# A two-block transformer kernel: the causal convolution by even and odd tokens, without matmuls

## The chip, the cores and the metric

One NeuronCore of one Trainium2 chip. The time is device microseconds of one execution; of a kernel the median of its runs is given. The engines are named as in the profile: PE is TensorE (PEld its weight loads), DVE is VectorE, ACT is ScalarE, POOL is GpSimd, SP only issues DMAs. The profile is one execution with its own time.

## The reference, cut to what matters

Two blocks over 1024 tokens of width 1024, float32. The first is the one that the change is about; each block ends in a convolutional feed-forward net, and the second has attention in place of these two branches.

```
h  = rms_norm(x, even_norm_g)
z  = h @ even_w_in + even_b_in                     # 1024 -> 4 * 512
za, zb = gelu(z[:, :1024]), z[:, 1024:]
# branch A: u, v = split(za); v = layer_norm(v); mixed = per head and 128-token chunk w_s @ v + b_s
ya = u * mixed
# branch B: a, g = split(zb)
c  = causal_dwconv(a * sigmoid(g), conv_w, conv_b) # 31 taps, one filter for each of 512 channels
yb = silu(layer_norm(c))
x  = x + concatenate([ya, yb], -1) @ even_w_out
```

## The kernel before

Every product is made three times, since each operand is split in a high and a low part (`split`: ACT casts the high part, DVE subtracts it): `mm3` issues high*high, high*low, low*high into one PSUM bank (`bank`, eight of them).

The order on every engine is the order in which the code issues. `Ticker` keeps a program time: a tick is called after every two k-steps, that is six matmuls of 512 columns, `after(n, fn)` issues `fn` n ticks later, and hooks run at each tick. An engine takes its own list in order and waits at each instruction for what it needs. `Meter` keeps a rough backlog of DVE and POOL, by a cost for each instruction and a credit for each tick.

`mix` is the first block's first half. Its stages on PE, in order:
1. `psu` for branch B: for each of four channel tiles c (128 channels each) the products for a and g; `done` makes `h` = (a + bias) * sigmoid(g), channels on partitions, 1024 tokens along the row.
2. `psv`: the products for v, token tile by token tile (`i` of 8); `v_chain` has the bias, gelu, layer norm and the split (`vn`, `vh`, `vl`).
3. `psu` for u, and between them `mix_pair(c)`: the mixing products (`psm`), bias on ACT (`mixed`), transposes (`pst`), `u * pst` on DVE, and the split into `ya`.
4. `psd`: `ya` times the first four row tiles of `w_out`, in two groups of two, each over 16 units (8 token tiles, 2 halves); DVE adds each finished bank to `x` (`x<-psd,x`).
5. `yb_chain`: transposes of the convolved channels (`psc`), layer norm, transposes back (`psb`), silu and split (`ybh`, `ybl`); then `psd` for the last four row tiles of `w_out`, and the norm of the feed-forward net (`psn`).

The 31 taps of the convolution run in the background of stages 1 to 4 (`background`, at each tick). A tap at distance s adds w * h, s tokens later, to `acc`:
- on DVE: one `scalar_tensor_tensor` on up to 1024 tokens, issued while DVE's backlog is below `slack`;
- by DMA: ACT multiplies (`tap`), and POOL's DMA queue adds the product to `sides` in HBM (an accumulating DMA); when a tile has all of them, `close` loads the sum (`side`), and POOL adds it to `acc`. `DMA_TAPS` = (6, 10, 9, 7) of each tile go this way;
- on PE: 12 taps of the last tile, as products with diagonal matrices (`diagonals`, `pe_taps`, tile `psk`), put into stage 2 ahead of token tile 2.

`yb_chain` is issued `YB_AT` ticks after the last convolution instruction is. `weights.take` hands out the split weights of a group and sets the splits of the next one.

## Time and profile before

| | |
|---|---|
| median of 3 runs | 2198.48 us (2198.35 to 2198.55) |
| profiled execution | 2198.7 us; its span 2197.0 us |
| PE busy | 2172.1 us, 99% of the span |
| DVE, ACT, POOL busy | 1591.7, 1094.8, 771.0 us (72, 50, 35%) |
| mean granted clock of PE | 0.998 of full |
| mean DMA rate | 164 GB/s |

Busy time is the union of an engine's instructions. Matmuls overlap: one of 512 columns is listed with about 390 ns, and the next starts 227 ns after it, so what one costs is read from start to start. `mix` takes the first 300 us.

### The profile page before, as it was taken

To read this page: it belongs to the slowest core of one execution; us is meant where nothing else is said; L and a number is where in the kernel's file an instruction comes from. 1 tells how busy PE (TensorE), PEld (TensorE's weight loads), DVE (VectorE), ACT (ScalarE), POOL (GpSimd) and SP (SyncE) were. 2 spreads that over 40 slices of the span, in tenths; PEclk is the share of its full clock that TensorE was granted. 3 is DMA by queue.
4 is the path that set the end of the run, shared out by engine and by line. 5 is a ranking of instruction groups with operands and counts; after the bars stand their busy time and mean duration, and the time that the engine had idled before them with its cause. 6 is when DMAs were issued, how large, how long until landed. Compare 5 with 4: busy or idle time off the path is not lost.

```text
span 2197.0 us, 29344 instructions
## 1 busy us (share of the span) xinstructions
PE 2172.1 (99%) x10496; PEld 1822.3 (83%) x10496; DVE 1591.7 (72%) x2551; ACT 1094.8 (50%) x1667; POOL 771.0 (35%) x561
## 2 busy tenths in 40 slices
PE   8999999999999999999999999999999999999998
PEld 7888788888888888888888888888888888888887
DVE  6998859877777775555777667776787777777556
ACT  5445455444444445254555655554654444444532
POOL 1122134766666330041112221211466666653001
PEclk9999999999999999999999999999999999999999
DMA  5569422434444597356344444743134444349933
GB/s 193 130 129 192 149 87 72 165 147 158 172 151 157 190 368 284 137 180 163 101 116 113 125 129 122 239 145 117 68 125 168 163 158 173 134 158 351 364 130 123
DMA packets 140850, 359.48 MB, mean 164 GB/s; under 512 B 16672, under 2 KB 17056, under 8 KB 140704
## 3 DMA queue, kind: packets, MB, share of 16 engines
q1 hardware_dynamic: 134512, 335.15, 45.0%
q0 software_dynamic: 5040, 18.27, 4.3%
q10 hardware_dynamic: 1152, 4.19, 0.5%
q8 instruction: 82, 1.34, 0.2%
q14 instruction: 64, 0.52, 0.1%
HBM read 219.68 MB, written 104.31 MB: 147 GB/s over the span
## 4 chain that ended last, share of the span: by engine, by line
PE 48%; issue 9%; DVE 2%; DMA 2%; ACT 2%; POOL 1%; SPq 1%; POOLq 0%; DVEq 0%; ACTq 0%
PE psd L1273 9%; PE psu L273 4%; PE psu L274 4%; PE psu L272 4%; PE psb L1093 3%; PE psb L1090 3%; PE psb L1091 3%; PE po L1594 3%; PE psc L1093 2%; PE psc L1090 2%; PE psc L1091 2%; PE ppt L1575 1%; PE pss L1508 1%; PE pss L1507 1%; PE ppt L1574 1%
## 5 line engine op out<-in xcount | busy, mean ns | idle before, releaser
L1273 PE MATMUL psd<-ab 128*128 128x512 f32 x1800 | 410.4, 390 | 0.0
L1273 PEld LDWEIGHTS psd<-ab 128*128 128x128 f32 x1800 | 337.6, 188 | 70.4 <-DVE ab L142 0.7
L272 PE MATMUL psu<-hTh,w 128*128 128x512 f32 (+1 forms) x608 | 239.9, 395 | 0.0
L273 PE MATMUL psu<-hTl,w 128*128 128x512 f32 (+1 forms) x608 | 232.1, 382 | 1.1 <-DVE hTl L142 1.1
L274 PE MATMUL psu<-hTh,w 128*128 128x512 f32 (+1 forms) x608 | 232.1, 382 | 0.0
L210 ACT CAST ab<-ab 128x1024 fp32r<-128x1024 f32 x150 | 156.0, 1051 | 140.3 <-PE psd L1273 54.5
L142 DVE TENSOR_TENSOR ab<-ab,ab 128x1024 fp32r<-128x1024 f32 x150 | 192.8, 1338 | 36.1 <-ACT ab L210 35.7
L142 DVE TENSOR_TENSOR x<-psd,x 128x512 f32<-128x512 f32 x152 | 101.5, 686 | 133.6 <-PE psd L1273 108.4
L142 POOL TENSOR_TENSOR y<-y,y 128x512 f32<-128x512 f32 x66 | 93.4, 1415 | 184.6 <-DMA act<-y 109.9
L1127 ACT COPY sn<-psb 128x512 f32<-128x512 f32 x120 | 70.4, 586 | 165.6 <-PE psb L1093 121.8
L142 DVE TENSOR_TENSOR tt<-ppt,tt 128x512 fp32r<-128x512 f32 (+1 forms) x160 | 101.4, 635 | 64.4 <-ACT tt L210 62.8
L210 ACT CAST tt<-ppt 128x512 fp32r<-128x512 f32 (+1 forms) x160 | 86.6, 541 | 113.4 <-PE ppt L1575 73.0
L274 PEld LDWEIGHTS psu<-hTh,w 128*128 128x128 f32 x608 | 115.1, 189 | 22.4
L273 PEld LDWEIGHTS psu<-hTl,w 128*128 128x128 f32 x608 | 115.6, 190 | 18.1 <-DVE hTl L142 1.9
L142 POOL TENSOR_TENSOR sm<-sm,mhalf 128x1 f32<-128x1 f32 (+2 forms) x38 | 33.2, 875 | 276.4 <-DVE sm L142 274.0
L272 PEld LDWEIGHTS psu<-hTh,w 128*128 128x128 f32 x608 | 115.5, 190 | 16.6 <-ACT hTh L210 0.2
L142 POOL MEMSET tt<- 128x256 f32 x64 | 19.8, 312 | 308.6 <-PE ppt L1575 110.5
L142 POOL TENSOR_TENSOR s<-wr 128x512 f32<-128x512 f32 x40 | 86.5, 2162 | 110.6 <-DVE psa L142 97.9
L142 DVE TENSOR_TENSOR wl<-wr,wh 128x1024 fp32r<-128x1024 f32 x88 | 116.0, 1318 | 0.5 <-ACT wh L210 0.5
L1594 PE MATMUL po<-tt,v 128*128 128x256 f32 x640 | 109.0, 292 | 4.0 <-DVE tt L142 4.0
L1524 ACT ACTIVATE p<-p,sma 128x896 f32<-128x896 f32 (+7 forms) x128 | 99.5, 778 | 25.6 <-DVE sma L142 25.0
L142 DVE TENSOR_TENSOR pse<-psc,sn 128x512 f32<-128x512 f32 x40 | 28.0, 699 | 115.6 <-ACT sn L1127 110.7
(252 smaller groups left out, 5896.2 us busy)
## 6 DMA issues: line engine op xcount, KB each, us to landing
wr<-in_w_up_dram SPq DMA_DIRECT2D x88, 512.0 KB, 4.3
ab<-act SPq DMA_DIRECT2D x154, 256.0 KB, 5.4
act<-y SPq DMA_DIRECT2D x66, 512.0 KB, 3.1
wq<-in_w_down_dram SPq DMA_DIRECT2D x44, 512.0 KB, 5.1
wt<-wq SPq DMA_DIRECT2D x44, 512.0 KB, 4.6
ab<-wt SPq DMA_DIRECT2D x88, 256.0 KB, 5.4
ab<-in_w_down_dram SPq DMA_DIRECT2D x66, 256.0 KB, 5.4
wr<-in_w_qkv_dram SPq DMA_DIRECT2D x24, 512.0 KB, 4.3
```

Of the source, the lines that this page charges most:

```text
L142: return fn(*args, **kw)
L210: nc.scalar.copy(hi, src)
L272: nc.tensor.matmul(out_ap, st[0], mv[0], start=first, stop=False)
L273: nc.tensor.matmul(out_ap, st[0], mv[1], start=False, stop=False)
L274: nc.tensor.matmul(out_ap, st[1], mv[0], start=False, stop=last)
L1090: nc.tensor.matmul(ps, st[0], mv[0], start=f, stop=False, skip_group_check=True)
L1091: nc.tensor.matmul(ps, st[0], mv[1], start=False, stop=False, skip_group_check=True)
L1093: nc.tensor.matmul(ps, st[1], mv[0], start=False, stop=e, skip_group_check=True)
L1127: nc.scalar.copy(self.sn[key], self.b)
L1273: nc.tensor.matmul(ps, a[:, c], b[:, HALF:D], start=first and k == 0, stop=last and k == 2, skip_group_check=True)
L1524: nc.scalar.activation(p, p, AF.Exp, bias=sm[:, 2:3], scale=0.125, accum_out=lsum[hp][:, c:c + 1])
L1594: nc.tensor.matmul(po[:, c], v2[:, kb, :], tt[:, z, 256 * n:256 * n + 256], start=(g == 0 and n == 0 and z == 0), stop=(g == j and n == 1 ...
```

## The change

The tokens of `h` are kept in two halves, even (h0) and odd (h1), and so are the taps: W0 at even distances (16), W1 at odd ones (15). With y0 = W0 * h0 and y1 = W1 * h1 in the two halves of `acc`, and cc = (W0 + W1) * (h0 + h1), the even outputs are y0 + y1 one step later, the odd ones cc - y0 - y1. Each filter runs over 512 tokens.
- y0 and y1: 29 taps for each tile on DVE (`tap`) and their first ones on ACT (`start`). The `acc` of three tiles is stored to HBM (`park`) and loaded again.
- cc: all 16 taps by DMA, two in one transfer of 512 KB (`send`), 8 transfers for each tile, as many in all as before (32). The sum is loaded by SP, and four DVE instructions put the output `y` together (`merge`), in place of POOL's addition.
- `pe_taps`, `diagonals` and their splits are gone.
- The mixing products are set by ticks (`MIX_AT`, `MIX_STEPS`), between the u's; ya's products are one group of four row tiles: half as many additions to `x`. Its first four units (`YA_HEAD`) do three of the four row tiles first.
- The two layer norm steps of a `vn` pair alternate; `Meter`'s numbers, slacks and weight splits are set anew, one of them in attention (`W_O_AT`).

What the change moves, at the three places that the prediction speaks of. PE, stage 2, after the products of token tile 1 (`psv`), before:

```order
L273 MATMUL psv_1042<-w_927,hTh_165 128x512
L274 MATMUL psv_1042<-w_927,hTl_166 128x512
L508 MATMUL psk_1077<-hh_984,dgh_745 128x512
L508 MATMUL psk_1077<-hl_985,dgh_745 128x512
L508 MATMUL psk_1077<-hh_984,dgl_746 128x512
L508 MATMUL psk_1077<-hh_984,dgh_745 128x510
```

PE at the same place after the change:

```order
L282 MATMUL psv_1099<-w_972,hTh_165 128x512
L283 MATMUL psv_1099<-w_972,hTl_166 128x512
L281 MATMUL psv_1138<-w_871,hTh_161 128x512
L282 MATMUL psv_1138<-w_871,hTh_161 128x512
L283 MATMUL psv_1138<-w_871,hTl_162 128x512
```

All 72 products of `psk` are gone, and the next token tile follows at once. PE, stage 4, ahead of the first `psc` (of the convolved channels `acc`, later `y`), before:

```order
L274 MATMUL psd_1976<-w_1674,ya_1717 128x512
L272 MATMUL psd_1976<-w_1759,ya_1814 128x512
L273 MATMUL psd_1976<-w_1759,ya_1814 128x512
L274 MATMUL psd_1976<-w_1759,ya_1814 128x512
L779 MATMUL psc_1986<-ident,acc_540 128x128
L779 MATMUL psc_1986<-ident,acc_665 128x128
L779 MATMUL psc_1986<-ident,acc_827 128x128
```

PE ahead of the first `psc` after the change:

```order
L281 MATMUL psd_2039<-w_1793,ya_1835 128x512
L282 MATMUL psd_2039<-w_1793,ya_1835 128x512
L283 MATMUL psd_2039<-w_1793,ya_1835 128x512
L862 MATMUL psc_2050<-ident,y_1736 128x128
L862 MATMUL psc_2050<-ident,y_1921 128x128
L862 MATMUL psc_2050<-ident,y_1962 128x128
L862 MATMUL psc_2050<-ident,y_2020 128x128
```

`psc` stood behind 60 of the 192 products of ya, and stands now behind 90. DVE, the last convolution instructions, before (the last tap is that on `acc_983`):

```order
L142 SCALAR_TENSOR_TENSOR acc_983<-h_907,cw_108,acc_983 128x996
L142 SCALAR_TENSOR_TENSOR acc_983<-h_907,cw_108,acc_983 128x995
L142 TENSOR_TENSOR x_1843<-psd_1850,x_1843 128x512
L142 SCALAR_TENSOR_TENSOR acc_983<-h_907,cw_108,acc_983 128x994
L142 TENSOR_TENSOR x_1843<-psd_1871,x_1843 128x512
L142 TENSOR_TENSOR w_1867<-wr_1703,w_1867 128x1024
```

DVE's last convolution instructions after the change (tile 3's `merge`, from `cc_1969` to `y_2020`):

```order
L151 TENSOR_TENSOR x_1773<-psd_1953,x_1773 128x512
L151 TENSOR_TENSOR x_1948<-psd_1988,x_1948 128x512
L151 TENSOR_TENSOR x_1948<-psd_2002,x_1948 128x512
L151 TENSOR_TENSOR cc_1969<-cc_1969 128x512
L151 TENSOR_TENSOR cc_1969<-acc_1243 128x512
L151 TENSOR_TENSOR y_2020<-acc_1243 128x511
L151 TENSOR_TENSOR y_2020<-cc_1969 128x512
L151 TENSOR_TENSOR x_1948<-psd_2024,x_1948 128x512
```

The taps ended on DVE among the first two additions to `x`, and POOL added the sums; now the last four instructions of `merge` stand behind six additions and wait for SP's load of `cc_1969`.

The diff, cut to its core:

```
-DMA_TAPS = (6, 10, 9, 7)
-PE_TAPS = 12
-PE_TAPS_AT = 2
-DIAG_AT = 40
+NP2 = (CONV_W + 1) // 2
+PAD = NP2
+DMA_PAIRS = (8, 8, 8, 8)
 DMA_PACE = 3
 CLOSE_AT = 6
 MERGE_STEPS = 6
-YB_AT = 3
-T_SLACK = 3.5
-DMA_STEPS = 8
+YB_AT = 2
+T_SLACK = 5.0
+DMA_STEPS = 6
...
-MIX_LAG = 8
+MIX_AT = 17
+MIX_STEPS = 4
+W_OUT_AT = (1, 4, 5, 6)
+W_OUT2_AT = (17, 20, 23, 26)
+YA_HEAD = 4
+YA_HI = 3
+BASE_AHEAD = 2
+PARK_AT = 2
+PARKED = 3
+LOAD_LEFT = (12, 8, 4, 2)
+W_O_AT = (1, 3, 11)
...
-            self.backlog += self.fixed + self.per_elem * n
+            fixed = self.fixed + 0.06 * (name == "scalar_tensor_tensor" or n < 64)
+            self.backlog += fixed + self.per_elem * n
...
-    vec = Meter(nc.vector, 0.12, 1.06e-3)
+    vec = Meter(nc.vector, 0.10, 1.05e-3)
     pool = Meter(nc.gpsimd, 0.12, 2.25e-3)
-    tk.hooks.append(lambda: (vec.step(1.28), pool.step(1.3)))
+    tk.hooks.append(lambda: (vec.step(1.36), pool.step(1.3)))
...
-        def take(self, spread, delay=0):
+        def take(self, spread, delay=0, at=None):
...
-                    after(1 + delay + i * spread, self.split_next)
+                    after(at[i] if at else 1 + delay + i * spread, self.split_next)
...
+        def part(u, js):
+            i, t = u
+            sl = slice(t * HALF, (t + 1) * HALF)
+            for j in js:
+                ah, al = acts[j]
+                a = ah(i), al(i)
+                if j == 0:
+                    banks[u] = bank("psd")
+                mm3(banks[u], a, (ws[j][0][:, sl], ws[j][1][:, sl]), j == 0, j == n - 1)
+                if j % 2 == 1 and j < n - 1:
+                    yield
+        def close(u):
+            i, t = u
+            sl = slice(t * HALF, (t + 1) * HALF)
+            ps = banks.pop(u)
+            after(1, lambda: vec.tensor_tensor(to[i][:, sl], ps, xs[i][:, sl], op=ALU.add))
+        for u in units[:head]:
+            yield from part(u, range(n - 1))
+            if n % 2 == 0:
                 yield
+        for m, u in enumerate(units[:head]):
+            yield from part(u, (n - 1,))
+            close(u)
+            if m % 2 == 1:
+                yield
+        for u in units[head:]:
+            yield from part(u, range(n))
+            close(u)
+            yield
+            if then is not None and u[1] == 1:
+                after(1, lambda i=u[0]: then(i))
...
+        accs, convs, cc_at, ccs, dma_todo, dma_last, dma_left = {}, {}, {}, {}, {}, {}, {}
+        conv_todo, merge_todo = deque(), deque()
+        slack = [2.0]
+        sides = dpool.tile([NC4, P, 2, HALF], F32, tag="sides", name="sides")
+        parks = dpool.tile([PARKED, P, 2, HALF], F32, tag="parks", name="parks")
...
+        class Conv:
+            def __init__(self, c):
+                self.c = c
+                self.h = stile([P, 2, HALF], name="h")
+                self.acc = None
+                self.todo = [(f, k) for k in range(1, NP2) for f in range(2) if 2 * k + f < CONV_W]
...
+            def add_phases(self):
+                c = self.c
+                t = stile(name="x2")
+                self.x2, self.ws, self.b2 = (t[:, a:b] for a, b in ((0, PAD + HALF), (D - NP2, D),
+                                                                    (D - NP2 - 1, D - NP2)))
+                pool.memset(self.x2[:, :PAD], 0.0)
+                pool.tensor_copy(self.ws[:, 0:1], cw[:, c, 0:1])
+                pool.tensor_tensor(self.ws[:, 1:], pairs[:, c, :, 0], pairs[:, c, :, 1], op=ALU.add)
+                pool.tensor_tensor(self.b2, cb[:, c:c + 1], cb[:, c:c + 1], op=ALU.add)
+                vec.tensor_tensor(self.x2[:, PAD:], self.h[:, 0, :], self.h[:, 1, :], op=ALU.add)
+            def start(self):
+                if self.acc is None:
+                    self.acc = stile([P, 2, HALF], name="acc")
+                    nc.scalar.activation(self.acc[:, 0, :], self.h[:, 0, :], AF.Identity,
+                                         bias=cb[:, self.c:self.c + 1], scale=self.weight(0, 0))
+                    nc.scalar.activation(self.acc[:, 1, :], self.h[:, 1, :], AF.Copy,
+                                         scale=self.weight(1, 0))
+            def tap(self):
+                self.start()
+                f, k = self.todo.pop(0)
+                t = self.acc[:, f, k:]
+                vec.scalar_tensor_tensor(t, self.h[:, f, :HALF - k], self.weight(f, k), t,
+                                         op0=ALU.mult, op1=ALU.add)
...
+            def park(self):
+                nc.gpsimd.dma_start(parks[self.c], self.acc)
+                self.acc = None
+            def send(self, n):
+                c, x2 = self.c, self.x2
+                t = stile([P, 2, HALF], name="tap")
+                for z in range(2):
+                    k = 2 * n + z
+                    bias = {"bias": self.b2} if k == 0 else {}
+                    nc.scalar.activation(t[:, z, :], x2[:, PAD - k:PAD - k + HALF],
+                                         AF.Identity if k == 0 else AF.Copy,
+                                         scale=self.ws[:, NP2 - 1 - k:NP2 - k], **bias)
                 def add():
+                    if n == 0:
                         nc.gpsimd.dma_start(sides[c], t)
                     else:
+                        nc.gpsimd.dma_start(sides[c], t, accum_op=ALU.add)
+                    dma_left[c] -= 1
                 after(1, add)
+            def merge(self, step):
+                y0, y1 = self.acc[:, 0, :], self.acc[:, 1, :]
+                q0, q1 = ccs[self.c][:, 0, :], ccs[self.c][:, 1, :]
...
+                elif step == 0:
+                    vec.tensor_tensor(q0, q0, q1, op=ALU.add)
+                elif step == 1:
+                    vec.tensor_tensor(q1, y0, y1, op=ALU.add)
+                elif step == 2:
+                    self.y = stile(name="y")
+                    self.out = self.y.rearrange("p (m f) -> p f m", f=2)
+                    nc.scalar.copy(self.out[:, 0, 0:1], y0[:, 0:1])
+                    vec.tensor_tensor(self.out[:, 0, 1:], y0[:, 1:], y1[:, :HALF - 1], op=ALU.add)
+                else:
+                    vec.tensor_tensor(self.out[:, 1, :], q0, q1, op=ALU.subtract)
+                    accs[self.c] = self.y
...
+        def queue_conv(cv):
+            cv.add_phases()
+            convs[cv.c] = cv
+            conv_todo.append(cv)
+            dma_todo[cv.c] = deque(lambda n=n: cv.send(n) for n in range(DMA_PAIRS[cv.c]))
+            dma_left[cv.c], dma_last[cv.c] = DMA_PAIRS[cv.c], tk.t
...
-            while conv_todo and vec.backlog < slack[0]:
-                conv_todo.popleft()()
+            for c in range(NC4):
+                if c not in cc_at and dma_left.get(c) == 0 and tk.t >= dma_last[c] + CLOSE_AT:
+                    left = sum(len(cv.todo) for cv in conv_todo)
+                    if left <= LOAD_LEFT[c] and len(merge_todo) <= 2:
+                        cc_at[c] = tk.t
+                        ccs[c] = stile([P, 2, HALF], name="cc")
+                        nc.sync.dma_start(ccs[c], sides[c])
+                        if c < PARKED:
+                            convs[c].acc = stile([P, 2, HALF], name="acc")
+                            nc.sync.dma_start(convs[c].acc, parks[c])
+                        steps = [-k for k in range(2 * DMA_PAIRS[c], NP2)] + list(range(4))
+                        merge_todo.extend((convs[c], step) for step in steps)
+                    break
+            while vec.backlog < slack[0] and sum(hT.done) == NT:
+                if merge_todo and tk.t >= cc_at[merge_todo[0][0].c] + MERGE_STEPS and not merge_todo[0][0].todo:
+                    cv, step = merge_todo.popleft()
+                    cv.merge(step)
+                elif conv_todo:
+                    cv = conv_todo[0]
+                    if len(cv.todo) <= BASE_AHEAD and len(conv_todo) > 1:
+                        conv_todo[1].start()
+                    cv.tap()
+                    if not cv.todo:
+                        conv_todo.popleft()
+                else:
+                    break
         tk.hooks.append(background)
...
-                    st["sig"], st["h"] = stile(name="sig"), stile(name="h")
+                    st["sig"], st["cv"] = stile(name="sig"), Conv(c)
                 nc.scalar.activation(st["sig"][:, sl], outs[(1, t)], AF.Sigmoid,
                                      bias=b_in[:, 12 + c:13 + c])
+                def phases(ap):
+                    return ap.rearrange("p (m f) -> p f m", f=2)
                 vec.scalar_tensor_tensor(
-                    st["h"][:, sl], outs[(0, t)], b_in[:, 8 + c:9 + c], st["sig"][:, sl],
+                    st["cv"].h[:, :, t * 256:(t + 1) * 256], phases(outs[(0, t)]),
+                    b_in[:, 8 + c:9 + c], phases(st["sig"][:, sl]),
                     op0=ALU.add, op1=ALU.mult)
                 if t == 1:
-                    queue_conv(c, st["h"])
+                    queue_conv(st["cv"])
...
+            def c():
+                for e in range(2):
+                    y = zs[:, e, :]
+                    vec.scalar_tensor_tensor(y, y, sm[:, 12 + 2 * e:13 + 2 * e], vgb[:, 0, :],
+                                             op0=ALU.subtract, op1=ALU.mult)
+                for e in range(2):
+                    y = zs[:, e, :]
+                    vec.scalar_tensor_tensor(y, y, sm[:, 22 + e:23 + e], vgb[:, 1, :],
+                                             op0=ALU.mult, op1=ALU.add)
...
-            if i == PE_TAPS_AT:
-                pe_taps()
...
-            after(MIX_LAG + 1, a)
-            after(MIX_LAG + 2, b)
-            after(MIX_LAG + 4, d)
-            after(MIX_LAG + 5, e)
+                def fin():
+                    yh, yl = hpair([P, S], "ya")
+                    hi_of(yh, u)
+                    after(1, lambda: lo_of(yl, u, yh))
+                    yas[c] = tok_view(yh, yl)
+                after(YA_HI if c < NC4 - 1 else 1, fin)
+            for n, fn in enumerate((a, b, None, d)):
+                if fn:
+                    after(MIX_AT + MIX_STEPS * c + n, fn)
+            return e
+        mixed_at = tk.t
+        ends = [mix_pair(c) for c in range(NC4)]
...
                 if t == 1:
-                    mix_pair(c)
-            ws = weights.take(2)
+                    after(max(1, mixed_at + MIX_AT + MIX_STEPS * c + 4 - tk.t), ends[c])
             if c < NC4 - 1:
+                ws = weights.take(2)
                 after(U_NEXT, weights.split_next)
+            else:
+                weights.lo_at = 1
+                ws = weights.take(0, at=W_OUT_AT)
+                load_x(0)
             drive(up_units(hT, ws, outs, done))
...
-        load_x(0)
-        for ks in ((0, 1), (2, 3)):
-            tk.until(lambda: all(k in yas for k in ks))
-            if ks[0] == 0:
-                for i in range(1, NT):
-                    after(max(1, 2 * i - X_AHEAD), lambda i=i: load_x(i))
-            down_group([yas[k] for k in ks], weights.take(4), xs)
+        for i in range(1, NT):
+            after(max(1, 4 * i - X_AHEAD), lambda i=i: load_x(i))
+        def ya_view(c):
+            def pick(part):
+                def view(i):
+                    tk.until(lambda: c in yas)
+                    return yas[c][part](i)
+                return view
+            return pick(0), pick(1)
+        down_group([ya_view(c) for c in range(NC4)], weights.take(0, at=W_OUT2_AT), xs, head=YA_HEAD)
...
-        return g + [rows(io["w_out"], ks) for ks in ((0, 1), (2, 3), (4, 5, 6, 7))]
+        return g + [rows(io["w_out"], ks) for ks in ((0, 1, 2, 3), (4, 5, 6, 7))]
```

More of the change, by code (lines that the diff above doesn't have):

```diff
@@ L444, in drive, with down_units @@
             tick()
-    def down_units(acts, ws, xs, then=None, to=None, tiles=range(NT)):
+    def down_units(acts, ws, xs, then=None, to=None, tiles=range(NT), head=0):
         to = to or xs
         n = len(ws)
-        for i in tiles:
-            for t in range(2):
-                sl = slice(t * HALF, (t + 1) * HALF)
-                ps = bank("psd")
-                for j in range(n):
-                    ah, al = acts[j]
-                    mm3(ps, (ah(i), al(i)), (ws[j][0][:, sl], ws[j][1][:, sl]),
-                        j == 0, j == n - 1)
-                    if j % 2 == 1 and j < n - 1:
-                        yield
-                after(1, lambda i=i, sl=sl, ps=ps: vec.tensor_tensor(
-                    to[i][:, sl], ps, xs[i][:, sl], op=ALU.add))
-                yield
-            if then is not None:
-                after(1, lambda i=i: then(i))
+        units = [(i, t) for i in tiles for t in range(2)]
+        banks = {}
+        def part(u, js):
[17 more added lines that the diff above has]
+            if n % 2 == 0:
+                yield
+        for m, u in enumerate(units[:head]):
[9 more added lines that the diff above has]
+                after(1, lambda i=u[0]: then(i))
     def down_group(*args, **kw):
@@ L473, in mix @@
     def mix(x_src, hT, then, late, begin):
-        accs, conv_todo = [], deque()
-        dma_todo, dma_last = {}, {}
-        left = [0]
-        slack = [1.1]
-        sides = dpool.tile([NC4, P, S], F32, tag="sides", name="sides")
-        pe = {}
-        def diagonals():
-            pe["d"] = []
-            for m0 in range(0, PE_TAPS, KT):
-                n = min(KT, PE_TAPS - m0)
-                d = stile([P, n, P], name="dg")
-                for m in range(n):
-                    j = CONV_W - 1 - 2 * (m0 + m)
-                    nc.scalar.activation(d[:, m, :], ident, AF.Copy,
-                                         scale=cw[:, NC4 - 1, j:j + 1])
-                dh, dl = (stile([P, n, P], F32R, name="dg" + z) for z in "hl")
-                after(3, lambda d=d, dh=dh, dl=dl: split(d, dh, dl))
-                pe["d"] += [(dh[:, m, :], dl[:, m, :]) for m in range(n)]
@@ L497, in pe_taps @@
-        def pe_taps():
-            hh, hl = pe["h"]
-            for t in range(2):
-                ps = bank("psk")
-                for m in range(PE_TAPS):
-                    s = 2 * m
-                    o = 0 if t else s
-                    rows = slice(t * HALF + o - s, (t + 1) * HALF - s)
-                    dh, dl = pe["d"][m]
-                    for n, (d, h) in enumerate(((dh, hh), (dh, hl), (dl, hh))):
-                        nc.tensor.matmul(ps[:, o:], d, h[:, rows],
-                                         start=m == 0 and n == 0,
-                                         stop=m == PE_TAPS - 1 and n == 2,
-                                         skip_group_check=True)
-                    if m % 2 == 1:
-                        tick()
-                nc.scalar.activation(accs[-1][:, t * HALF:(t + 1) * HALF], ps, AF.Identity,
-                                     bias=cb[:, NC4 - 1:NC4])
-            conv_todo.extend(pe["taps"])
@@ L543, in add @@
                 def add():
-                    if start:
+                    if n == 0:
                         nc.gpsimd.dma_start(sides[c], t)
                     else:
-                        nc.gpsimd.dma_start(sides[c][:, s:], t[:, :S - s], accum_op=ALU.add)
-                    if not dma_todo[c]:
-                        after(CLOSE_AT, close)
+                        nc.gpsimd.dma_start(sides[c], t, accum_op=ALU.add)
+                    dma_left[c] -= 1
+                if n == NP2 // 2 - 1:
+                    self.free()
@@ L550, in dma_tap @@
                 after(1, add)
-            def close():
-                t = stile(name="side")
-                nc.sync.dma_start(t, sides[c])
-                def merge():
-                    pool.tensor_tensor(acc, t, acc, op=ALU.add)
-                    left[0] -= 1
-                after(MERGE_STEPS, merge)
-            def dve_tap(j):
-                s = CONV_W - 1 - j
-                vec.scalar_tensor_tensor(
-                    acc[:, s:], h[:, :S - s], cw[:, c, j:j + 1], acc[:, s:],
-                    op0=ALU.mult, op1=ALU.add)
@@ L840, in conv_finished @@
         def conv_finished():
-            return not left[0] and not conv_todo
+            return all(c in accs for c in range(NC4))
         started = []
@@ L1484, in prepare @@
             if hp:
-                yield from project([rv], [fin_v])
+                yield from project([rv], [fin_v], W_O_AT if hp == KT - 1 else None)
             else:
```

80 lines of the change are left out of this document (30 added, 50 removed).

## The prediction

> **What bounds the kernel now.** I read the page's busy times first, then the windows of the first 300 us, where the change is made, then PE's and DVE's timelines there.
>
> ```profile
> PE 2172.1 (99%) x10496; PEld 1822.3 (83%) x10496; DVE 1591.7 (72%) x2551; ACT 1094.8 (50%) x1667; POOL 771.0 (35%) x561
> ```
>
> PE is busy in 99% of the span. The windows (PE busy and count, PEld, DVE, ACT, POOL, granted clock, DMA share, GB/s) show the same for the stages that change, from branch B's products to ya's:
>
> ```profile
> core 0: us, PE busy (x) PEld busy (x) DVE busy (x) ACT busy (x) POOL busy (x), PEclk, DMA share, GB/s
> 120.00:150.00 30.00, 30.00 (x133) 24.74 (x132) 28.85 (x39) 12.21 (x21) 9.95 (x9) 1.00 0.69 141
> 180.00:210.00 30.00, 30.00 (x138) 24.96 (x137) 25.33 (x34) 20.84 (x31) 9.59 (x11) 1.00 0.96 180
> 210.00:240.00 30.00, 29.43 (x147) 24.50 (x146) 25.19 (x27) 7.84 (x11) 9.18 (x4) 1.00 0.85 290
> ```
>
> 133 matmuls of 512 columns fill 30 us at 120 to 150, at full clock, with no idle time. So the stage's limit is the number of matmuls, and DVE is close behind: 28.85 of 30 us there, 25 later. Two things therefore decide: how much PE work goes, and whether DVE, with its new work, keeps PE fed in the shorter stage. Time won or lost here reaches the end one for one, since PE runs on as one queue.
>
> **PE.** The 72 products of the 12 diagonal taps, from the first of `psk` to the `psv` behind them (start, duration):
>
> ```profile
> 110.60 0.39 PE L272 MATMUL psv<-w,hTh 128*128 128x512 f32 x1
> ...
> 121.48 0.39 PE L508 MATMUL psk<-hh,dgh 128*128 128x512 f32 x1
> ...
> 137.99 0.39 PE L272 MATMUL psv<-w,hTh 128*128 128x512 f32 x1
> ...
> 193.79 0.39 PE L272 MATMUL psm<-vh,ws 128*128 128x512 f32 x1
> ```
>
> They take 137.99 - 121.48 = 16.5 us, and nothing else of PE's is removed or added: mixing products, transposes and the 192 products of ya only change places. One matmul is (121.48 - 110.60) / 48 = 0.227 us. So PE term: **-16.5 us**. The small stalls around `yb_chain` can also move:
>
> ```profile
> 235.95 1.03 PE L779 MATMUL psc<-ident,acc 128*128 128x128 f32 x8
> 237.55 0.50 PE L272 MATMUL psd<-w,ya 128*128 128x512 f32 x1 [0.57 <-DVE x L142]
> ...
> 239.05 1.04 PE L779 MATMUL psc<-ident,acc 128*128 128x128 f32 x8
> 239.84 0.47 PE L272 MATMUL psd<-w,ya 128*128 128x512 f32 x1
> ...
> 247.12 0.39 PE L274 MATMUL psd<-w,ya 128*128 128x512 f32 x1
> 248.22 1.32 PE L779 MATMUL psc<-ident,acc 128*128 128x128 f32 x8 [0.72 <-ACT yn L803]
> ...
> 276.82 0.39 PE L272 MATMUL psd<-w,ybh 128*128 128x512 f32 x1
> ```
>
> Eight transposes without a stall take 0.8 us (239.05 to 239.84), so 0.8 us is lost at 236 and 1.10 - 0.23 = 0.9 us at 247, where a bank is not yet free. Half as many additions to `x` free banks sooner for the first; the second, ACT's `yn`, stays. I take **-0.5 us** (bounds -1.7 and 0).
>
> **DVE, the cover that may fail.** What DVE does from 57.18 us (an `h` that waits for PE, so that the queue is empty) to the last tap's end, and the taps in it:
>
> ```profile
> core 0: us, PE busy (x) PEld busy (x) DVE busy (x) ACT busy (x) POOL busy (x), PEclk, DMA share, GB/s
> 57.18:190.62 133.44, 133.44 (x590) 110.40 (x588) 124.60 (x170) 65.25 (x104) 30.98 (x35) 1.00 0.65 138
> 57.18:226.78 169.60, 169.60 (x761) 140.65 (x760) 155.10 (x197) 84.00 (x127) 39.56 (x42) 1.00 0.73 161
> ...
> core 0: us, DVE busy (x), PEclk, DMA share, GB/s
> 57.18:190.62 133.44, 76.35 (x59) 1.00 0.65 138
> 57.18:226.78 169.60, 98.32 (x75) 1.00 0.73 161
> ```
>
> The first two rows are all instructions, the last two the 59 and 75 taps alone (`acc`). The prices, start to start, are in these rows of DVE's timeline:
>
> ```profile
> 68.19 0.74 DVE L142 SCALAR_TENSOR_TENSOR h<-psu,b_in,sig 128x512 f32<-128x512 f32 x1
> 68.85 2.56 DVE L142 SCALAR_TENSOR_TENSOR acc<-h,cw,acc 128x1007 f32<-128x1007 f32 x2
> ...
> 113.39 1.23 DVE L142 TENSOR_TENSOR hl<-h,hh 128x1024 fp32r<-128x1024 f32 x1
> 114.53 2.55 DVE L142 SCALAR_TENSOR_TENSOR acc<-h,cw,acc 128x1002 f32<-128x1002 f32 x2
> ...
> 122.02 1.23 DVE L142 SCALAR_TENSOR_TENSOR acc<-h,cw,acc 128x998 f32<-128x998 f32 x1
> 123.17 0.68 DVE L142 TENSOR_TENSOR vn<-psv,vbi 128x512 f32<-128x512 f32 x1
> ...
> 131.55 2.98 DVE L142 SCALAR_TENSOR_TENSOR vn<-vn,sm,vgb 128x512 f32<-128x512 f32 x4
> 134.45 2.58 DVE L142 SCALAR_TENSOR_TENSOR acc<-h,cw,acc 128x1013 f32<-128x1013 f32 x2
> ...
> 230.35 1.27 DVE L142 TENSOR_TENSOR x<-psd,x 128x512 f32<-128x512 f32 x2
> 231.55 0.67 DVE L142 TENSOR_TENSOR u<-pst,u 128x512 f32<-128x512 f32 x1
> ```
>
> A 512-element `scalar_tensor_tensor` costs 0.66 us where the next is independent of it (`h`) and 2.90 / 4 = 0.725 where pairs depend (`vn`). The new taps have 497 to 511 elements and alternate between the halves, so each depends on the one before the last: 0.65 to 0.725, and I take 0.69. A 512-element addition costs 1.20 / 2 = 0.60, a 1024-element subtraction 1.14. A listed tap overlaps its successor by 0.08 us (1.23 against 1.15), so the 75 old ones are 98.3 - 6.0 = 92.3 us.
> The sum up to the last `merge`: 155.1 - 92.3 - 2.9 (the splits of `h`, 1.14, and of the diagonals, 1.14 + 0.60) + 111 new taps (116 without the five ahead of 57 us) at 0.65 to 0.725 = 72.2 to 80.5, + three sums h0 + h1 (1.8), + 16 `merge` instructions (9.6), + what was behind `psc` and is now ahead of it: two weight splits, two splits of ya, four u's, five additions to `x` (2.3 + 2.3 + 2.4 + 3.0). That makes 153.5 to 161.8 us, so DVE's end is at 210.7 to 219.0 us without idle time; before it idled 169.6 - 155.1 = 14.5 us, largely in waits that a later DVE would not have. The order puts the first `psc` behind 30 more products of ya and one more group of 8 transposes (0.8 us): 235.95 - 16.5 + 6.8 + 0.8 = 227.0 us. Bounds: DVE is 8 to 16 us early without idle time, and with all of the old idle time 1.8 us early to 6.5 us late. An earlier date is the first `psm`, at 193.79 - 16.5 = 177.3, which needs the last `vl`. Same working on the first rows, with 92 new taps for 59 old ones (71.6 us): 124.6 - 71.6 - 2.9 + 1.8 + 59.8 to 66.7 = 111.7 to 118.6, so 168.9 to 175.8 us, plus idle time. Of that the largest piece is
>
> ```profile
> 183.13 0.36 DVE L142 TENSOR_TENSOR sm<-sm 128x2 f32<-128x2 f32 x2 [3.99 <-POOL sm L142]
> ```
>
> a wait for POOL in `v_chain`, which moves with `psv` to 166.6. What stood behind it ended by 190.62, 7.5 us later; with two more taps, less the longer old one, that is 8.4 us, so it ends at 175.0, ahead of 177.3. So I take a stall of **+1.5 us** in all, with 0 and +7 as ends. The layer norm's alternating order is in the price of `vn`, and nothing more.
>
> [...]
>
> **ACT, POOL, SP and the DMAs.** For each transfer ACT does two multiplications of 512 instead of one of 1024, and for each tile two first taps:
>
> ```profile
> L541 ACT ACTIVATE tap<-h,cw 128x1024 f32<-128x1024 f32 x28 | 31.9, 1147 | 10.1 <-DMA sides<-tap 7.4 <-PE psk L508 2.7
> L721 ACT ACTIVATE mixed<-psm,bs 128x512 f32<-128x512 f32 x8 | 5.0, 679 | 0.0
> L142 POOL TENSOR_TENSOR acc<-side,acc 128x1024 f32<-128x1024 f32 x4 | 12.6, 3168 | 13.5 <-DMA side<-sides 7.4 <-DVE acc L142 6.1
> ```
>
> At 0.68 each that is 32 * (1.36 - 1.15) = +7 us; the window above has ACT at 84 of 169.6 us, which hides it. POOL loses its 12.6 us of additions and gets 16 instructions of one or a few columns and three stores (`park`), which only tile loads wait for; it is at 39.6 of 169.6 us. SP issues 7 loads instead of 4. The DMAs:
>
> ```profile
> side<-sides SPq DMA_DIRECT2D x4, 512.0 KB, 5.9
> ...
> sides<-tap POOLq DMA_DIRECT2D x3, 511.0 KB, 5.0
> ...
> 192.15 0.86 POOL L547 DMA_DIRECT2D sides<-tap  x1 [3.30 <-ACT tap L541]
> ...
> 209.18 0.86 POOL L547 DMA_DIRECT2D sides<-tap  x1 [1.71 <-ACT tap L541]
> ```
>
> A load lands in 5.9 us; `MERGE_STEPS` leaves it six ticks (6 * 6 * 0.227 = 8.2 us), so DVE finds it there. The six accumulations from 192 to 209 us were issued 3.4 us apart, and the new pace is at least three ticks, 4.1 us. Six transfers more (three stores, three loads), in a stage with a DMA share of 0.73: hidden, and I take 0. The later split of one weight in attention (`W_O_AT`) is ACT work at 50% busy: 0.
>
> **Sum.** -16.5 - 0.5 + 1.5 = -15.5 us. The profiled execution, 2198.7 us (span 2197.0), would be 2183.2; it lies 0.2 us above the median of 2198.48, so **2183.0 us**.
>
> **Rivals.**
> (a) DVE comes late: taps at 0.725 and the old idle time in full make 7 us at `psc`, and a 2 to 5 us tail by banks that wait for its additions: a stall of 7 to 12 us in place of 1.5, 2189 to 2194 us. For it: DVE at 28.85 of 30 us. Against: the waits that go when DVE is late, and POOL's additions, 3.2 us each, next to which taps were slow.
> (b) The slower side: the accumulating DMAs queue up. 32 sends and three stores from about 62 us (the tile's last `h` comes after 57.18) at p us each end at 62 + 35 p; then 5.9 for the load and 2.4 for `merge`, against 227.0. From p = 4.95 on the stall is more than 16.5 us; at 5.2, about what one takes to land, it is 25.3, and the time 2198.5 - 16.5 + 25.3 = 2207. For it: a share of 0.96 at 180 to 210 us. Against: the six issues 3.4 us apart, each landing in about 5, so they overlap.
> [...]
> (d) The stage is set by something else that fills the gap, so that no more than 4 us is won: 2194 to 2198. PE's 30.00 of 30 us speaks against it.
>
> **Chances.** Forecast 0.64 (own range 2179 to 2187), (a) 0.17, (b) 0.06, (c) 0.08, (d) 0.05. What a measurement tells from no change is about 0.2%, 4.4 us: faster means below 2194.1. Faster: 0.64 + 0.08 + 0.13 of (a) = 0.85; slower 0.06; the same 0.09, of (a)'s end and (d). The range from 2179 (all stalls gone, -1.7, DVE in time, and about 1 us of what the rows can't show) to 2191 (a stall of 9 us) holds the forecast, (c) and about half of (a), 0.8.
>
> **What would show it.** No `psk`; first `psm` near 177 us, first `psc` near 227, first product of `ybh` near 259 (276.8 before); taps at 0.65 to 0.72 start to start; DVE's last `y` before 227; no PE wait on DVE over 2 us there. Wrong if PE waits for `vl`, `y` or banks by more than 5 us, or for `cc` behind a late DMA.

## The result, and the profile after

| | before | after |
|---|---|---|
| median, same chip, 5 runs each | 2198.55 us (2198.35 to 2202.46) | 2178.58 us (2178.19 to 2179.47) |
| ratio | | 0.9905, 95% interval 0.9890 to 0.9919 |
| span of the profiled execution | 2197.0 us | 2177.0 us |

The kernel is 20.0 us faster, 4.4 us more than predicted and 0.4 us below the low end of the range. The page's busy times, and of its DMA issues the accumulating ones:

```profile
PE 2153.9 (99%) x10424; PEld 1807.7 (83%) x10424; DVE 1562.9 (72%) x2591; ACT 1096.9 (50%) x1691; POOL 768.7 (35%) x572
...
sides<-tap POOLq DMA_DIRECT2D x32, 512.0 KB, 6.4
```

PE has 72 matmuls and 18.2 us less, DVE 28.8 us less, in more instructions; a `sides` transfer lands in 6.4 us (median) where it took 5.2, and neither PE nor DVE waits for one. Where the time went is read from the starts of PE's stages. Of the changed kernel (start, duration, line), from the first `psv` to the last product; `psd<-w,o` is the first product of attention's output weight `w_o`:

```profile
111.76 0.39 PE L281 MATMUL psv<-w,hTh 128*128 128x512 f32 x1
...
178.40 0.39 PE L281 MATMUL psm<-vh,ws 128*128 128x512 f32 x1
...
228.28 0.38 PE L862 MATMUL psc<-ident,y 128*128 128x128 f32 x2
...
259.49 0.39 PE L281 MATMUL psd<-w,ybh 128*128 128x512 f32 x1
...
277.18 0.49 PE L386 MATMUL psn<-ident,xn 128*128 128x128 f32 x3
...
1399.18 0.40 PE L281 MATMUL psd<-w,o 128*128 128x512 f32 x1
...
2168.41 0.39 PE L1353 MATMUL psd<-abh,abl 128*128 128x512 f32 x1
```

Of the kernel before, those of the same starts that the prediction does not show:

```profile
294.51 0.38 PE L377 MATMUL psn<-ident,xn 128*128 128x128 f32 x2
...
1419.58 0.63 PE L272 MATMUL psd<-w,o 128*128 128x512 f32 x1
...
2188.74 0.39 PE L1273 MATMUL psd<-abh,abl 128*128 128x512 f32 x1
```

The differences, and the same of all kernels run below (us, one profiled execution of each):

| kernel | first psv | psv to psm | psm to ybh | ybh to psn | psn to w_o | w_o to last |
|---|---|---|---|---|---|---|
| before | 110.60 | 83.19 | 83.03 | 17.69 | 1125.07 | 769.16 |
| after | 111.76 | 66.64 | 81.09 | 17.69 | 1122.00 | 769.23 |
| before_ticks | 111.08 | 83.20 | 82.34 | 17.69 | 1120.92 | 768.73 |
| before_o_behind | 110.56 | 83.19 | 84.03 | 17.69 | 1121.99 | 768.74 |
| even_again | 111.23 | 66.65 | 81.07 | 17.69 | 1122.21 | 769.50 |
| even_nudged | 112.17 | 66.64 | 81.02 | 17.68 | 1125.31 | 769.92 |
| after_nudged | 111.28 | 66.64 | 81.02 | 17.68 | 1121.41 | 770.38 |
| before_diag_out | 110.66 | 77.43 | 90.90 | 17.68 | 1122.54 | 769.13 |
| products_back | 111.02 | 82.96 | 84.59 | 17.68 | 1123.31 | 769.06 |
| taps_8 | 111.97 | 66.64 | 80.38 | 18.71 | 1121.56 | 769.26 |
| taps_16 | 112.11 | 66.64 | 85.83 | 24.47 | 1120.28 | 769.21 |
| taps_24 | 111.53 | 66.64 | 90.92 | 22.72 | 1120.47 | 769.62 |
| ya_two | 111.22 | 66.64 | 83.62 | 17.68 | 1121.42 | 769.35 |
| norm_old | 110.90 | 66.64 | 81.09 | 17.69 | 1120.80 | 769.83 |

So from before to after: +1.2 up to the first `psv` (it varies from 110.56 to 112.17, see below), -16.55 where `psk` was, -1.94 up to the first `ybh` product, and -3.07 in a part that ends 1100 us later, together -20.3. (That last part, `psn` to `w_o`, varies from 1120.3 to 1123.3 where the stall told below is absent, so the 3.07 is known to some 1.5 us only.)

Nearly all of the +1.2 arises before 20 us, where PE has the same products in both kernels: in the profiled execution of before, products of 256 columns follow each other every 0.213 us up to 17.5 us and every 0.119 us behind, in that of after the slow ones go on to 19.8 us. In norm_old, which has the code of after up to there, they end at 18.0 us. So most of the +1.2 is no part of the change. One execution each of products_back, taps_16, ya_two and of the kernel before beside the first two took over 2700 us; the ratios leave these out, and the medians, which hold them, are at most 0.4 us too high.

The change from `psn` to `w_o` has a row among PE's waits (total, times, longest); before:

```profile
PE po L1594 <- DVE tt L142: 4.0, 3, 3.2
...
PE psc L779 <- ACT yn L803: 0.7, 1, 0.7
PE psd L272 <- DVE x L142: 0.6, 1, 0.6
```

and after:

```profile
PE po L1674 <- DVE tt L151: 1.6, 3, 0.9
...
PE psb L896 <- ACT yn L886: 0.3, 1, 0.3
```

The long wait for `tt` (the split of attention's transposed weights) is gone, and of those around `yb_chain` 0.3 us is left. What DVE does in the new stage, from its timeline:

```profile
58.29 0.75 DVE L151 SCALAR_TENSOR_TENSOR h<-psu,b_in,sig 128x512 f32<-128x512 f32 x1 [3.78 <-ACT sig L661]
...
80.72 9.95 DVE L151 SCALAR_TENSOR_TENSOR acc<-h,cw,acc 128x511 f32<-128x511 f32 x15
...
130.76 2.73 DVE L151 SCALAR_TENSOR_TENSOR vn<-vn,sm,vgb 128x512 f32<-128x512 f32 x4
...
226.93 0.68 DVE L151 TENSOR_TENSOR y<-cc 128x512 f32<-128x512 f32 x1
```

A tap is (9.95 - 0.08) / 15 = 0.658 us, `h` at a step of two costs what it did (0.75 against 0.74), and the last `y` ends at 227.6, 0.7 us ahead of the first `psc`.

### The profile page after: what moved, and what is told of

The parts are those of the page before. It is cut to its first block, busy times and chain, and to the rows that moved or that the text cites. A ratio compares the mean times of both kernels' runs of the same rounds, so it can differ in the third digit from the quotient of the medians.

```text
span 2177.0 us, 29264 instructions
## 1 busy us (share of the span) xinstructions
PE 2153.9 (99%) x10424; PEld 1807.7 (83%) x10424; DVE 1562.9 (72%) x2591; ACT 1096.9 (50%) x1691; POOL 768.7 (35%) x572
## 4 chain that ended last, share of the span: by engine, by line
PE 82%; issue 9%; DVE 3%; ACT 2%; DMA 2%; POOL 1%; SPq 1%; POOLq 0%; DVEq 0%; ACTq 0%
PE psd L1353 10%; PE psu L282 7%; PE psu L283 7%; PE psu L281 7%; PE psb L1173 7%; PE psb L1171 7%; PE psb L1170 7%; PE psc L1171 3%; PE psc L1173 3%; PE psc L1170 3%; PE po L1674 3%; PE psa L1171 2%; PE psa L1173 2%; PE psa L1170 2%; PE psd L283 2%
## 5 line engine op out<-in xcount | busy, mean ns | idle before, releaser
L151 DVE TENSOR_TENSOR x<-psd,x 128x512 f32<-128x512 f32 x136 | 91.5, 687 | 137.0 <-PE psd L1353 106.3
```

What stands on the lines that cost most here:

```text
L151: return fn(*args, **kw)
```

## The experiments: the stall near 1416 us

Theory W: the new ticks `W_O_AT` removed a stall of the kernel before. In that kernel, PE, POOL and DVE there, and two windows (their columns are those of the prediction; the last three are granted clock, DMA share, GB/s):

```profile
1416.96 0.91 PE L1594 MATMUL po<-tt,v 128*128 128x256 f32 x3 [3.24 <-DVE tt L142]
...
1410.62 2.41 POOL L142 TENSOR_TENSOR w<-wr,w 128x1024 fp32r<-128x1024 f32 x1 [4.94 <-ACT w L210]
1412.99 2.36 POOL L142 TENSOR_TENSOR o<-o,r 128x1024 fp32r<-128x1024 f32 x1
...
1413.18 3.25 DVE L142 TENSOR_TENSOR rl<-rq,rh 128x1024 fp32r<-128x1024 f32 x1 [0.29 <-POOL w L142]
...
1413.30:1416.90 3.60, 0.41 (x4) 0.22 (x2) 3.60 (x3) 2.67 (x6) 2.30 (x2) 1.00 1.04 402
1416.90:1420.70 3.80, 3.74 (x14) 3.52 (x15) 2.90 (x7) 0.74 (x2) 0.00 (x0) 0.55 1.02 379
```

`tt` stands behind `rl` on DVE, and `rl` took 3.25 us where a subtraction of 1024 elements takes 1.2. It started 0.19 us behind POOL's `o` and ended 1.1 us after it. PE waited 3.24 us, and had 0.55 of its clock for 3.8 us more. In the changed kernel POOL has `o` ahead of its `w`, and it is nearly over when `rl` starts:

```profile
1393.23 2.40 POOL L151 TENSOR_TENSOR o<-o,r 128x1024 fp32r<-128x1024 f32 x1 [4.02 <-ACT r L219]
...
1395.29 1.43 DVE L151 TENSOR_TENSOR rl<-rq,rh 128x1024 fp32r<-128x1024 f32 x1
```

Four kernels were run together on one chip, where the kernel before had 2199.26 us.

**even_again**, the changed kernel with the old ticks:

```
-yield from project([rv], [fin_v], W_O_AT if hp == KT - 1 else None)
+yield from project([rv], [fin_v], None)
```

> The changed kernel with the weight splits of the last pair's value projection at ticks 1, 5 and 9 again. Theory W (the new ticks removed a stall of the old kernel near 1416 us): PE waits 3.2 us for a tt of DVE again, the granted clock drops to about 0.55 for some 4 us behind it, and the time rises by 5.1 us, to 2183.7. Rival S (the stall went because the earlier stages moved against the transfers, not because of the ticks): 2178.6, no wait above 1 us there. Rival H (the wait returns, the clock stays): 2181.8.

Measured: 2179.9 us (2178.6 to 2180.78), ratio 0.9912 (0.9898 to 0.9925). Theory W fails here: the stall does not come back. POOL and DVE:

```profile
1395.72 3.37 POOL L151 TENSOR_TENSOR o<-o,r 128x1024 fp32r<-128x1024 f32 x1
...
1395.54 1.31 DVE L151 TENSOR_TENSOR rl<-rq,rh 128x1024 fp32r<-128x1024 f32 x1
```

The same two instructions meet, but `rl` is first by 0.18 us, and now it is POOL's `o` that takes 1 us longer than its 2.4. From `psn` to `w_o` this run takes 1122.21 us, after 1122.00: so in the changed kernel the ticks gain nothing that these runs can tell from noise. The stall is gone there without them, as rival S has it.

**before_ticks**, the old kernel with the new ticks alone:

```
-yield from project([rv], [fin_v])
+yield from project([rv], [fin_v], (1, 3, 11) if hp == KT - 1 else None)
```

> The old kernel with only the new ticks (1, 3, 11) for these three splits; the convolution is the old one. Theory W: the 3.2-us wait of PE and the slow products behind it go, 2198.5 - 5.1 = 2193.4. Rival S: 2198.5. Rival H: 2195.3.

Measured: 2194.82 us (2193.32 to 2195.78), ratio 0.998 (0.9971 to 0.9989), 4.4 us less where theory W gave 5.1. In this kernel the ticks do remove the stall: POOL's `o` now comes ahead of its `w` (at 1409.18, for 2.41 us), and `rl` meets only its last 0.35 us, as in after. DVE:

```profile
1411.24 1.43 DVE L142 TENSOR_TENSOR rl<-rq,rh 128x1024 fp32r<-128x1024 f32 x1
```

**before_o_behind**, the old kernel with only POOL's `o` moved away:

```
-after(O_LOW if hp < KT - 2 else O_LOW_LAST, low)
+after(14 if hp == KT - 3 else O_LOW if hp < KT - 2 else O_LOW_LAST, low)
```

> The old kernel, with POOL's subtraction for the output of one pair (o <- o, r, 2.36 us at 1412.99) put behind two more POOL instructions, so that it does not run beside DVE's rl; the order of the three splits is the old one. Theory P (rl took 3.25 us instead of 1.23 because POOL worked beside it): rl takes 1.2 us, PE's wait falls from 3.2 to 1.2 us, the clock stays at 1.00, and the time falls by 2.0 + 1.7 = 3.7 us, to 2194.8. Rival Q (rl is slow, or DVE is late, for another reason, such as the order on ACT): rl stays at 3.2 us and the time at 2198.5.

Measured: 2196.46 us (2195.09 to 2200.13), ratio 0.9989 (0.998 to 0.9998). DVE and PE:

```profile
1414.21 1.23 DVE L142 TENSOR_TENSOR rl<-rq,rh 128x1024 fp32r<-128x1024 f32 x1 [0.30 <-POOL w L142]
...
1415.96 0.63 PE L1594 MATMUL po<-tt,v 128*128 128x256 f32 x3 [1.22 <-DVE tt L142]
```

Both as theory P has them, 1.23 and 1.22 us, and the next 5 us ran at a clock of 1.00. The time fell by 2.8 us rather than 3.7; in the table 3.1 us are won in this part, and 1.0 lost between `psm` and `ybh`, which this edit does not touch.

If the order of two starts decides, 0.4 us of delay must bring the stall back. Two kernels on another chip (before: 2200.48 us), **even_nudged** and **after_nudged**, with three tiny DVE instructions ahead of `rl` of the last pair, the first on even_again, the second on the changed kernel:

```
+late = smpool.tile([P, 2], F32, ...)
+nc.vector.memset(late, 1.0)
+for _ in range(2):
+    nc.vector.tensor_scalar_mul(late, late, 1.0)
 lo_of(st["rl"], raw(), st["rh"])
```

> The changed kernel with the old ticks of the three splits (as in even_again), and three tiny DVE instructions, about 0.4 us together, ahead of rl of the last pair. In even_again rl started 0.18 us ahead of POOL's o and was not slowed; in the kernel before it started 0.19 us behind and took 3.25 us. Theory R (whoever reads first holds the other off): rl now starts behind o, takes about 3.2 us, PE waits some 3.3 us (0.94 + 0.4 + 2.0) and runs at half clock for some 3.5 us behind it; 2179.9 + 4.1 = 2184.0. Rival N (the order does not matter; rl was slow in the kernel before for another reason): rl takes 1.3 us, PE waits 1.4 us, 2180.3.

> The changed kernel itself (with the new ticks), and the same three tiny DVE instructions ahead of rl. POOL's o stands there 2 us ahead of rl and its w behind it, so theory R expects no long block: rl 1.2 to 1.5 us, no wait of PE above 1 us near 1397 us, 2178.6. Rival K (any delay of DVE at this place costs): 0.4 us more at least, and if POOL's w gets in ahead of rl some 4 us, 2179.0 to 2182.7.

Measured: 2183.51 us (2182.04 to 2183.61), ratio 0.9923 (0.9909 to 0.9936), and 2178.02 us (2176.58 to 2178.65), ratio 0.9898 (0.9885 to 0.9912). In even_nudged:

```profile
1397.31 2.35 POOL L151 TENSOR_TENSOR o<-o,r 128x1024 fp32r<-128x1024 f32 x1
...
1397.26 2.67 DVE L1479 TENSOR_SCALAR late<-late 128x2 f32<-128x2 f32 x2
1399.60 1.21 DVE L151 TENSOR_TENSOR rl<-rq,rh 128x1024 fp32r<-128x1024 f32 x1
...
1401.34 0.62 PE L1683 MATMUL po<-tt,v 128*128 128x256 f32 x3 [3.33 <-DVE tt L151]
...
1400.00:1404.00 4.00, 2.66 (x17) 2.46 (x18) 3.50 (x7) 1.03 (x3) 0.00 (x0) 1.00 1.02 413
```

and in after_nudged:

```profile
1394.04 0.44 DVE L1479 TENSOR_SCALAR late<-late 128x2 f32<-128x2 f32 x2
```

The stall is back, and it is the two tiny instructions that were held, 2.67 us in place of 0.44 (the first starts 0.05 us ahead of `o`; the second, by an estimate from the 0.44 us for both, 0.1 to 0.2 us behind it); PE waits the 3.3 us that were expected, though at full clock. With the new ticks the same delay costs nothing. So theory R holds, but for the half clock that it expected: whichever started later was held, DVE by 2.0 us in before (3.25 for 1.23) and 2.2 in even_nudged, POOL by 1.0 in even_again (3.37 for 2.41). The ticks take the two apart; without them the changed kernel happened to have the better order.

## The experiments: PE's products and DVE's time

**before_diag_out**, the old kernel with 2 of the 72 `psk` products left (on the chip of the first three):

```
 for n, (d, h) in enumerate(((dh, hh), (dh, hl), (dl, hh))):
-    nc.tensor.matmul(ps[:, o:], d, h[:, rows], start=m == 0 and n == 0, ...)
+    if m == 0 and n == 0:
+        nc.tensor.matmul(ps[:, o:], d, h[:, rows], start=True, stop=True, ...)
```

> The old kernel with 70 of the 72 products of the diagonals left out (two are left to fill the two banks), so that 12 taps of one tile are missing; DVE, ACT, POOL and the DMAs do what they did. Theory of the prediction's first term: 70 x 0.227 = 15.9 us less, 2182.6, as the stage is set by the number of matmuls. Rival D (DVE, at 28.85 of 30 us, becomes the limit of the shorter stage): PE waits for DVE before the first psc, and only some 5 to 12 us go: 2186 to 2193.

Measured: 2198.03 us (2196.49 to 2200.24), ratio 0.9995 (0.9986 to 1.0004): nothing is won, less even than rival D gave. The long wait is ahead of `psm`, not of `psc`. PE's waits, and the windows from the first `psv` to `psm` and on to `ybh`:

```profile
PE psm L272 <- ACT vh L210: 7.9, 1, 7.9
PE pst L731 <- ACT mixed L721: 3.6, 1, 3.6
...
110.70:188.10 77.40, 67.81 (x298) 55.19 (x296) 71.92 (x119) 38.54 (x66) 22.75 (x24) 0.96 0.71 137
188.10:279.00 90.90, 86.22 (x403) 70.53 (x404) 74.55 (x108) 44.52 (x57) 15.35 (x11) 0.94 0.59 163
```

In the kernel before and in the changed one the same two windows are:

```profile
110.60:193.80 83.20, 83.20 (x368) 68.79 (x367) 76.23 (x129) 41.80 (x71) 24.55 (x25) 1.00 0.74 142
193.80:276.80 83.00, 81.57 (x403) 67.27 (x402) 71.84 (x98) 41.13 (x51) 15.50 (x10) 1.00 0.59 166
```

```profile
111.80:178.40 66.60, 66.60 (x295) 55.16 (x294) 64.70 (x140) 41.52 (x84) 18.60 (x24) 1.00 0.84 176
178.40:259.50 81.10, 80.76 (x404) 67.32 (x403) 57.76 (x94) 42.28 (x59) 7.17 (x7) 1.00 0.59 181
```

DVE (third number) has 148.1 us of work in the 166.2 us before, and 146.5 of it stay without `psk`, nearly all of the 150 us that would be left. The changed kernel gives DVE 122.5 us, 25.6 us less. That this is why the old kernel wins nothing is argued, not shown. From 111 to 178 us DVE is busy for 65.0 of 67 us here, for 64.5 in before, and for 65.1 in the changed kernel, where PE waits for nothing: the taps fill what time there is. And the edit keeps the ticks of the products that it leaves out, so the taps that are issued at these ticks still stand ahead of `v_chain` on DVE, in less time. What the old kernel would win with its taps set anew for the shorter stage, no run shows.

**products_back**, the changed kernel with 72 products put back, one token tile behind the place of `psk` (before on this chip: 2201.22 us):

```
+if i == 3:
+    for t in range(2):
+        ps = bank("psk")
+        ... 36 products of 512 columns, a tick after every six
 ps = bank("psv")
```

> The changed kernel with 72 products of 512 columns put back at the place where psk stood, between the third and the fourth psv group; their result is used by nobody. Theory O (PE's products count one for one as long as DVE keeps up): psv to psm 66.6 + 16.4 = 83.0 us, and the time 2178.6 + 16.4 = 2195.0. Rival G (the new stage has a hidden limit, DVE or the DMAs, that would take up part of it): psv to psm 70 to 80 us, 2182 to 2192.

Measured: 2198.36 us, ratio 0.9987 (0.9978 to 0.9996). `psv` to `psm` is 82.96 us, 16.3 more: one for one, as theory O has it for this stage. 3.5 us more were lost up to `ybh`, half of them by a wait and half by the clock behind it:

```profile
235.41 1.32 PE L871 MATMUL psc<-ident,y 128*128 128x128 f32 x8 [1.81 <-ACT yn L895]
...
235.40:240.30 4.90, 4.87 (x21) 4.00 (x22) 1.81 (x3) 1.97 (x3) 0.00 (x0) 0.65 0.00 0
```

How much DVE could be late was asked with taps done twice, in three kernels (before: 2199.46 us on the chip of **taps_8** and **taps_24**, 2201.22 on that of **taps_16**; k % 8 for 8, k in (4, 8) for 16, k % 4 for 24):

```
-vec.scalar_tensor_tensor(t, self.h[:, f, :HALF - k], self.weight(f, k), t, ...)
+for _ in range(2 if k % 8 == 0 else 1):
+    vec.scalar_tensor_tensor(t, self.h[:, f, :HALF - k], self.weight(f, k), t, ...)
```

> The changed kernel with 8 of its DVE taps done twice (two for each tile, so these count double in the sum): 8 x 0.66 = 5.3 us more for DVE. Theory L (DVE, busy 113.6 of the 118 us up to the first psm, is nearly the limit of the new stage): about 4 us of it before the first psm, which uses up the idle time; PE waits 0 to 3 us, 2178.6 to 2181.6. Rival M (the slack is some 8 us or more, as the prediction had it without idle time): no change, 2178.6, first psm at 178 us.

> The same with 24 taps done twice: 15.7 us more for DVE, some 13 of them ahead of the first psm. Theory L: 113.6 + 13 is 9 us more than the 118 us there are; PE waits 6 to 12 us for vl or y, and behind a wait of over 3 us the granted clock drops; 2186 to 2192. Rival M: DVE's work only moves into the 18.6 us in which it idles up to 228 us; up to 2 us more, 2178.6 to 2180.6.

> The changed kernel with 16 DVE taps done twice, 10.5 us more. Theory C (the cover of a late DVE are the ya products: in the changed kernel 31.2 us lie between the first psc and the first product of ybh, and the chain needs 18 of them, so psc may slide by some 13 us): psc slides by 22.9 x 10.5 / 15.7 = 15.3 us to about 243.6, 2 us too late; PE waits 2 to 3 us in all, the clock stays at 1.00, 2181. Rival F (every us of DVE beyond its idle time counts): in proportion to the 15.2 us of the run with 24, from 8 on, some 7 us: 2186.

Measured: taps_8 2178.44 us (2177.86 to 2178.77), ratio 0.9905 (0.9892 to 0.9919), no change; taps_24 2193.77 us (2191.8 to 2194.18), 0.9972 (0.9961 to 0.9982); taps_16 2188.78 us, 0.9943 (0.993 to 0.9956). The first `psm` stays where it was in all three (66.64), so the wait that theory L expected ahead of it does not come; nor does rival M's 2180.6 for 24 taps. What slides is the first `psc`, to 233.90 with 8, 243.59 with 16 and 251.14 with 24, since the taps are issued as the backlog allows; PE runs ya's products meanwhile and has none left when the chain is due. In taps_24 PE's waits are

```profile
PE psd L281 <- ACT ybh L219: 5.4, 2, 5.1
PE psb L897 <- ACT yn L887: 4.1, 4, 3.6
...
258.90:264.00 5.10, 4.46 (x16) 3.18 (x16) 3.00 (x7) 5.07 (x7) 0.00 (x0) 0.50 0.11 43
```

and in taps_16

```profile
264.58 0.80 PE L281 MATMUL psd<-w,ybh 128*128 128x512 f32 x1 [5.74 <-ACT ybh L219]
...
265.00:275.00 10.00, 9.64 (x29) 6.31 (x29) 2.70 (x3) 4.82 (x8) 0.00 (x0) 0.58 0.01 2
```

Theory C had the place of `psc` to 0.1 us and the price too low (about 10 us in place of 2.4): from `psc` to `ybh` are 21.0 us there, not 18, and 10 us at 0.58 of the clock cost 4.2 more. So, as an estimate, the first `psc` could come some 10 us later (31.2 us to `ybh` in the changed kernel less these 21.0), about 7 us of DVE's work (10.5 of it moved `psc` by 15.3), and behind that a wait can be paid again in clock, as here at 0.58.

**ya_two**, the changed kernel with ya's products in two groups (so without the head of four units, and with a line, not shown here, by which `x` is loaded every two ticks for each tile and not every four), and **norm_old**, with the layer norm's old order (both on the chip of taps_8):

```
-down_group([ya_view(c) for c in range(NC4)], weights.take(0, at=W_OUT2_AT), xs, head=YA_HEAD)
+ws = weights.take(0, at=W_OUT2_AT)
+for ks in ((0, 1), (2, 3)):
+    down_group([ya_view(k) for k in ks], [ws[k] for k in ks], xs)
```

```
 for e in range(2):
     y = zs[:, e, :]
     ... (op0 subtract, op1 mult)
-for e in range(2):
-    y = zs[:, e, :]
     ... (op0 mult, op1 add)
```

> The changed kernel with the ya products in two groups again: the same 192 products, but 16 additions to x in place of 8. Theory A (half as many additions free the banks sooner, which removed the small stalls around yb_chain): the 1.9 us return, 2180.5, with waits of PE for x or yn of 0.5 to 1 us each; DVE has 8 x 0.6 us more. Rival T (the stalls went because the start of yb_chain, one tick earlier, stands better against the products): 2178.6, no wait over 0.4 us.

> The changed kernel with the layer norm's four multiplications per pair of rows in the old order (two that depend on each other, then the other two). Theory: a group of four costs 2.98 us in place of 2.73, four groups 1.0 us of DVE's time ahead of the first psm, which its idle time there (4.4 us) still covers: no change, 2178.6. Rival (no slack is left in v_chain): the first psm is 0.25 to 1 us later, 2179 to 2179.6.

Measured: ya_two 2180.54 us, ratio 0.9915 (0.9901 to 0.9928); norm_old 2177.65 us (2177.0 to 2179.82), 0.9904 (0.989 to 0.9917), no change, with groups of 2.98 us for 2.73, as expected. In ya_two `psm` to `ybh` is 2.5 us longer than after, by

```profile
PE psd L281 <- DVE x L151: 1.5, 3, 1.0
...
PE psc L862 <- ACT yn L886: 0.6, 1, 0.6
```

waits for the same two as in the kernel before. In time the intervals of ya_two and after still overlap; on its own chip its 2179.88 to 2181.18 us lie above all of taps_8 (2177.86 to 2178.77). Theory A fits, and rival T does not; but since three things were undone together, that it is the number of additions is not shown apart from the head and the loads.

## Why the prediction was right and wrong

- **PE term, -16.5:** -16.55, and PE is busy in 66.60 of the 66.60 us; products_back gives 16.3 for the same 72 products put back. It does not follow from the products alone: before_diag_out, with the old taps at the old ticks, wins nothing.
- **Stalls around `yb_chain`, -0.5 (bounds -1.7 and 0):** mis-sized, -1.94. The working kept the wait for ACT's `yn` ("the second, ACT's `yn`, stays"); it fell from 0.72 to 0.3 us, and was 0.6 again in ya_two. Both stalls together were 1.7 us; the rest of the 1.94 has no row that shows it.
- **DVE late, +1.5 (0 to +7):** mis-sized, 0. A tap cost 0.658, not 0.69, so 116 of them 3.7 us less; and the place of `psc` is not fixed against DVE, as the working took it: the order moves it with DVE's backlog.
- **Behind `mix`, 0:** the step that failed. The prediction let all that follows move along unchanged ("Time won or lost here reaches the end one for one"), and put `W_O_AT` at 0 by ACT's share of busy time, in a stage whose timeline was not read; the row [3.24 <-DVE tt] stood in the profile of before. The runs show 3.07 us won there, since the stall is gone: which of POOL's `o` and DVE's `rl` starts first has changed. Without these 3.07 us the time would have been some 2181.7 us, inside the range. In the old kernel the new ticks alone are worth 4.4 us; in the changed one the stall stays away without them too (even_again), by 0.18 us between two starts, which is luck; with them it stays away even when DVE is 0.4 us later (after_nudged).
- **Sum:** -16.55 - 1.94 - 3.07 = -21.6, +1.2 of the start, most of it not the change's; the end behind the last product is 0.3 us longer. The low end, 2179, counted the stalls near the change, and about 1 us for what no row showed.
- **The rivals:** (a) DVE late did not come, and taps_16 shows what it would have cost; (b) no wait of PE for `cc` or `y`; (c), a slow `h` at a step of two, has 0.08 of the chances, and no run shows it: 0.75 us against 0.74; (d) the stage followed PE.
- **The marks:** `psm` 178.4 for 177, `psc` 228.3 for 227, `ybh` 259.5 for 259, the first two late by the start's 1.2.

The trace has the hold in both directions, 3.25 us for 1.23 and 3.37 for 2.41, but not for every pair: in before the `tt` instruction beside POOL's `w` was not slowed (at 1410.64, 0.55 us, as elsewhere). That `tt` has one input in PSUM, where `rl` and `o` have none; whether that is the reason, no run here shows.
